# A token-major input stage, planned on five engines, in a two-layer diffusion block

## The chip, the core and the metric

The kernel runs on one core of a Trainium2 chip. Its time is the device time of one launch in microseconds (us). TensorE (PE) multiplies matrices and accumulates in PSUM; VectorE (DVE), ScalarE (ACT) and GpSimd (POOL) work on tiles in SBUF and PSUM; SyncE (SP) issues most of the loads. The profile gives, beside busy times, the clock that was granted to TensorE, as a share of full speed.

## The reference

There are 512 latent tokens `x` and 256 context tokens `ctx`, each of 1024 float32 features, and two layers. Layer 0 mixes tokens by bidirectional retention, layer 1 by HGRN2; each is followed by a convolutional GLU. What the change touches is the entry of layer 0:

```python
mod_l = silu(c) @ ada_w[0] + ada_b[0]            # shift, scale, gate, shift, scale, gate
u_l = rms_norm(x, norm_g[0, 0]) * (1 + sc1_l) + sh1_l      # and the same for ctx with c_ctx
q, k, v, g = split(u @ w_in, [1024, 2048, 4096])           # 4 heads; dk 256, dv 512
q, k = axial_rope(q), axial_rope(k)                        # latent tokens only; k scaled by 1/16
log_gamma = log_sigmoid(decay)                             # per direction and head
# chunkwise recurrence with gamma, forward and backward, context first, then
# group norm of each head, silu(g) times it, and w_out
```

Here `rms_norm` divides each token by the root of its mean square and multiplies by a gain for each feature.

## The kernel before

Activations lie feature-major: a tile has 128 features on the partitions and tokens along the free axis, in 8 feature blocks. The 768 tokens are three chunks of 256: two of latent tokens (0 and 1), then the context (2). A float32 operand is split into a high half rounded to the multiplier's format (`hi`, written by ACT) and the rest (`lo`, the operand minus `hi`, written by DVE or POOL; `split`, L93 and L94). A product is then three matmuls: hi by hi, lo by hi, hi by lo (`mm3g`, L121).

The **input stage** is what runs before the retention of head 0. SP issues its loads in program order; big ones are 1 MB each: four blocks of the scale's weights (`rada`, 1_0 to 1_3), three chunks of the transposed input `hT` (`hcin`), two blocks of the query and key weights of head 0 (`rrl`), four blocks of the shift's weights (`rada`, 0_0 to 0_3), two of the value weights of head 0 (`rv`).

- A block of the modulation vector is a PE product with silu(c) (`ada`, L216), an ACT copy to rows (L218), a PE turn to columns (`adat`, L240) and the bias (L223). From the four scale blocks DVE makes the factor `mv0A` (L341).
- A chunk is squared on ACT (L366) and summed on DVE (L368, L371); a matmul with ones sums over the features (`npshin`, L131); the reciprocal root comes from ACT (L137) and is refined on DVE (L142 to L144). DVE and POOL multiply the chunk by it (L377), ACT multiplies by `mv0A` and writes hi (L384), DVE writes lo (L385).
- The first query and key products (`ld`, L121, 288 matmuls 128x256) are made from this scaled chunk, without the shift. The shift's share of q and k is the shift times the weights (`wb`, L687, turned by `wbt`, L694), added where q and k leave PSUM: with the rotary factors for latent tokens (L780, then L781 on POOL), by ACT for the context (L792).
- Later the chunk is made again with the shift for the value product (POOL L507, then split to `ua` by L93 and L94), and the value product follows (`v`, L819, six blocks of 128 tokens with 24 matmuls each: blocks 0 and 1 read chunk 0, blocks 2 and 3 chunk 1, blocks 4 and 5 the context).

The retention then needs decay strips `T` (L742 to L754): a ramp from POOL, an exponential on ACT with the log of gamma, a mask and an addition on POOL. The log comes out of a chain of small operations on `ret_decay` (`small_params`, L174 to L207). The first consumer is `pm` on DVE (L860), scores times strip; its halves `ph` and `pl` feed the PE product `av` (L870).

In this stage ACT's order is written by hand; the orders of DVE and PE come from a scheduler that lists what the program text offers at hooks between the products, and SP is in program order. POOL's is the scheduler's too. From the retention on everything is listed by that scheduler.

A class `Plan` orders another stage already: steps with an engine, a cost, dependences and a rank go one by one to the engine that is free first on the plan's own clock, and are emitted in that order.

## Time and profile before

| | us |
|---|---|
| median of 3 runs (2180.42 to 2181.96) | 2181.53 |
| the profiled execution | 2182.16 |
| its span, first to last instruction | 2180.4 |
| PE busy | 2117.5 |
| DVE busy | 1344.1 |
| ACT busy | 832.3 |
| POOL busy | 304.3 |

The span and the profiled execution differ by 1.76 us of start and end. Mean granted clock over the span is 0.991. In the views a row of a group has its line, engine, operation, out<-in, count, busy time and mean duration in ns, and last the idle time of the engine ahead of it with what ended it; a row of a timeline has its start, its length, and the same names. Overlapping matmuls of one row are counted from the first start to the last modelled end, so a matmul's own pace is read from the distance between starts.

### The profile page before, as it was taken

What the parts mean: (1) busy time and instruction counts of PE and PEld (TensorE: products, weight loads), DVE (VectorE), ACT (ScalarE), POOL (GpSimd) and SP (SyncE); (2) the same over time, 40 slices, a digit from 0 to 9 for tenths busy, and PEclk for the clock granted to TensorE, in tenths of its full rate; (3) what the DMA queues carried; (4) which work ended last, traced back from release to release, by engine and by line L of the source; (5) the groups of instructions that cost most, each with busy time, mean ns of one, the idle gap of its engine ahead of it and who ended that gap; (6) DMA issues with size and microseconds to landing.
All of it is one profiled execution on the core that took longest, in us unless ns stands there. A gap on an engine that the chain in (4) does not pass through costs nothing. (4 is left out here: it accounts for less than half of the span.)

```text
span 2180.4 us, 30973 instructions
## 1 busy us (share of the span) xinstructions
PE 2117.5 (97%) x12416; PEld 1787.0 (82%) x12416; DVE 1344.1 (62%) x2536; ACT 832.3 (38%) x1615; POOL 304.3 (14%) x383
## 2 busy tenths in 40 slices
PE   6999999999899999999999999999999889999997
PEld 5888888888788988788888889888888668888886
DVE  6867665673523667477577576777777764334445
ACT  4543343423513633323122155434443454333323
POOL 4622040220100000000000003333333310000000
PEclk9999999999999999999999999999999999999999
DMA  9122314233133233333333532212121243232232
GB/s 296 40 77 91 113 44 141 66 119 125 40 106 116 89 116 106 111 115 118 120 113 121 188 98 86 59 40 59 40 59 40 78 167 117 94 99 97 92 112 97
DMA packets 186608, 218.25 MB, mean 100 GB/s; under 512 B 6112, under 2 KB 157664, under 8 KB 185696
## 3 DMA queue, kind: packets, MB, share of 16 engines
q1 hardware_dynamic: 179280, 196.80, 27.8%
q0 software_dynamic: 2736, 13.11, 1.6%
q10 hardware_dynamic: 4448, 6.35, 0.8%
q8 instruction: 98, 1.61, 0.3%
q14 instruction: 46, 0.38, 0.1%
HBM read 200.90 MB, written 15.34 MB: 99 GB/s over the span
## 5 line engine op out<-in xcount | busy, mean ns | idle before, releaser
L121 PE MATMUL f<-um,hua 128*128 128x512 f32 (+1 forms) x960 | 258.2, 356 | 0.0
L121 PE MATMUL f<-um,huv 128*128 128x512 f32 (+1 forms) x960 | 255.8, 354 | 0.0
L264 DVE SCALAR_TENSOR_TENSOR rows<-rada,sc,rows 128x256 f32<-128x256 f32 x504 | 231.9, 485 | 5.4
L1069 PE MATMUL f<-hd,gt 128*128 128x512 f32 x720 | 228.3, 396 | 0.0
L121 PEld LDWEIGHTS f<-um,hua 128*128 128x128 f32 x960 | 169.6, 189 | 29.4 <-issue 4.0
L121 PE MATMUL hp<-ue,hhw 128*128 128x512 f32 (+1 forms) x672 | 192.1, 373 | 0.0
L121 PEld LDWEIGHTS f<-um,huv 128*128 128x128 f32 x960 | 170.1, 189 | 25.3
L121 PE MATMUL f<-um,lua 128*128 128x512 f32 (+1 forms) x480 | 170.0, 354 | 0.0
L121 PE MATMUL f<-um,luv 128*128 128x512 f32 (+1 forms) x480 | 169.7, 354 | 0.0
L1069 PEld LDWEIGHTS f<-hd,gt 128*128 128x128 f32 x720 | 134.9, 187 | 33.6 <-issue 0.8
L1069 PE MATMUL f<-ld,gt 128*128 128x512 f32 x360 | 142.2, 395 | 0.0
L121 PEld LDWEIGHTS hp<-ue,hhw 128*128 128x128 f32 x672 | 111.9, 189 | 17.8 <-issue 1.4
L819 PE MATMUL v<-hv,ua 128*128 128x512 f32 x384 | 120.5, 390 | 0.0
L121 PE MATMUL hp<-ue,lhw 128*128 128x512 f32 (+1 forms) x336 | 120.1, 357 | 0.0
L121 PEld LDWEIGHTS f<-um,lua 128*128 128x128 f32 x480 | 90.7, 189 | 12.9
L121 PEld LDWEIGHTS f<-um,luv 128*128 128x128 f32 x480 | 90.7, 189 | 12.6
L1041 DVE TENSOR_TENSOR c<-f,c 128x512 f32<-128x512 f32 (+1 forms) x60 | 36.1, 602 | 100.9 <-PE f L121 100.8
L995 PE MATMUL wo<-hwo,ogr 128*128 128x512 f32 x288 | 89.4, 391 | 1.8 <-ACT ogr L93 1.6
L1028 ACT ACTIVATE c<-f,c_conv_b,c_conv_w 128x512 f32<-128x512 f32 (+1 forms) x60 | 42.1, 703 | 117.4 <-PE f L121 117.4
L819 PEld LDWEIGHTS v<-hv,ua 128*128 128x128 f32 x384 | 72.1, 188 | 15.4 <-issue 0.6
L94 DVE TENSOR_TENSOR lua<-rua,hua 128x512 fp32r<-128x512 f32 x80 | 50.6, 686 | 53.8 <-ACT hua L93 53.6
L451 POOL DMA_DIRECT2D h_dram<-hxe x6 | 3.2, 533 | 576.2 <-DVE yf L421 542.5
(483 smaller groups left out, 4851.9 us busy)
## 6 DMA issues: line engine op xcount, KB each, us to landing
rada<-ada_w SPq DMA_DIRECT2D x48, 1024.0 KB
rua<-ffn_w_up SPq DMA_DIRECT2D x20, 1024.0 KB
ruv<-ffn_w_up SPq DMA_DIRECT2D x20, 1024.0 KB
rd<-ffn_w_down SPq DMA_DIRECT2D x24, 768.0 KB
rhw<-hg_w_in SPq DMA_DIRECT2D x28, 512.0 KB
rv<-ret_w_in SPq DMA_DIRECT2D x8, 1024.0 KB
rg<-ret_w_in SPq DMA_DIRECT2D x8, 1024.0 KB
rqk<-ret_w_in SPq DMA_DIRECT2D x6, 1024.0 KB
```

The lines of the kernel that those rows point to most:

```text
L94: (eng or self.nc.vector).tensor_tensor(lo, raw, hi.bitcast(F32), ALU.subtract)
L121: nc.tensor.matmul(o, a, b[:, s], start=(i == 0), stop=(i == n - 1))
L264: nc.vector.scalar_tensor_tensor(rows[:, v], raw[:, k], a, rows[:, v], ALU.mult, ALU.add)
L451: nc.vector.tensor_tensor(hb(b), hb(b), yb(b), ALU.add), nc.gpsimd.dma_start(hdst[ts], hb(b))))
L819: nc.tensor.matmul(ps, a, b, start=(c == 0 and k == 0 and z == 0), stop=(c == 1 and k == 3 and z == 2))
L995: nc.tensor.matmul(ps, l, r[:, k], start=(h == 0 and k == 0 and z == 0), stop=(h == 2 and k == 3 and z == 2))
L1028: nc.scalar.activation(c[:, s], ps, AF.Identity, bias=cb[:, i, mt : mt + 1], scale=w(1))
L1041: nc.vector.tensor_tensor(c[:, s], ps, c[:, s], ALU.mult)
L1069: nc.tensor.matmul(ps, l, r[:, k], start=(k1 + k == 0 and z == 0), stop=(k1 + k == nt - 1 and z == 2))
```

## The change

The three chunks are loaded from the token-major input `h` (tokens on the partitions, rows of 4 KB); `hT` is no longer an input. The sum of squares of a token is then along the free axis: ACT squares a block of 128 tokens with an accumulated sum (L626) and takes the reciprocal root (L630), DVE refines it on one column and multiplies the identity by it (L150 to L152, L635). PE turns the chunk to feature-major by multiplying with this diagonal, which scales each token too: twelve "crosses" of four float32 matmuls 128x128 (`tri`, L653). ACT and DVE read the halves from PSUM with the factor `mv0A` (L659, L681). The matmuls with ones and the multiplications L377 go.

The context chunk gets scale and shift at once (L665, split by L671 and L675), and needs no second making. For the latent chunks the shifted version is made on DVE from the finished halves, hi + lo + shift (L778), and split again (ACT L783, DVE L784); POOL does none of it. The lo halves of the weights are all DVE's (L616, L804); POOL had taken 10 of those 16. POOL keeps the rotary additions (L871) and the strips.

All of the input stage, the rotary part and the splits of the value weights are steps of one plan over SP, PE, ACT, DVE and POOL. Steps that write one of the two small PSUM banks hold it until the step that reads it frees it. The factor `mv0A` is made in four pieces, so a chunk's first features can go ahead of the last scale block. `small_params` is called after the plan; the rotary tables are loaded through POOL's queue.

```diff
-    def run(self):
-        free = {"PE": 0.0, "ACT": 0.0, "DVE": 0.0, "SP": 0.0}
+    def run(self):
+        free = {"SP": 0.0, "PE": 0.0, "ACT": 0.0, "DVE": 0.0, "POOL": 0.0}
...
+                can = [s for s in can if not s.hold or len([t for t in back if t > now]) < self.banks]
...
-        self.fold, self.ada_b, self.norm_g, self.sel = (self.const(c) for c in ("fold", "ada_b", "norm_g", "sel"))
-        self.rsel, self.ident = self.const("rsel"), self.const("ident")
...
         nc.scalar.activation(self.sc[:, :, 0:2], cT, AF.Silu)
+        self.fold, self.ident, self.ada_b, self.norm_g, self.sel, self.rsel = (
+            self.const(c) for c in ("fold", "ident", "ada_b", "norm_g", "sel", "rsel"))
...
-    def norm_in(self, nm, chunk, hsrc, mods, u, big, tmp, late):
...
+    def first(self, u, big, tmp, rot, flat):
+        plan = Plan(2)
...
+        for n, (f, *a) in enumerate(((get_a, 1, 0), (get_x, 0), (get_w, 0), (get_a, 1, 1), (get_w, 1), (get_a, 1, 2),
+                                     (get_a, 1, 3), (get_x, 1), *((get_a, 0, c) for c in range(4)), (get_x, 2))):
+            loads[(f, *a)] = add("SP", 2.9, [], (n,), lambda f=f, a=a: f(*a))
...
+            def square():
+                ss.append(self.cp.tile([P, 1], F32, tag="iss", name=f"iss{p}{b}", bufs=6))
+                nc.scalar.activation(xs[p][:, 2], xs[p][:, b], AF.Square, accum_out=ss[0])
...
+            def diag():
+                dg.append(self.cp.tile([P, P], F32, tag="diag", name=f"idg{p}{b}", bufs=4))
+                self.newton(r[0], ss[0])
+                nc.vector.tensor_scalar(dg[0], self.ident, r[0][:, 0:1], None, ALU.mult)
...
+                def cross(j=j, ps=ps):
+                    ps.append(self.sml(f"tri{p}{j}").rearrange("p (f t) -> p f t", f=2))
+                    for f in range(2):
+                        for b, (_, dg) in enumerate(ready):
+                            k = 2 * j + f
+                            nc.tensor.matmul(ps[0][:, f, b * P : b * P + P], xs[p][:, b, k * P : k * P + P], dg[0],
+                                             start=True, stop=True)
...
+                t = add("PE", 0.45, [n for n, _ in ready] + [scale[j]] + [shift[j]] * v, (0, p, j), cross, 0.2, hold=True)
...
+                def whole(j=j, x=x):
+                    x.append(tmp(f"lt{p}{j}").rearrange("p (f t) -> p f t", f=2))
+                    for f in range(2):
+                        k = 2 * j + f
+                        h, l = self.uhl(u, k, cs)
+                        nc.vector.scalar_tensor_tensor(x[0][:, f], l.bitcast(F32), bs[:, k, v : v + 1], h.bitcast(F32),
+                                                       ALU.add, ALU.add)
...
+                n = add("DVE", 0.95, lead[p] + shift, (1, 4 + p, j), whole)
...
-            self.setup()
-            rope = []
-
-            def extra():
-                rope.extend(self.const(c, pool=rp, eng=nc.sync) for c in ("rope_row", "rope_col"))
-                self.small_params(tmp)
...
-            self.first(u, big, tmp, extra, part)
+            with tc.manual_schedule(engines={mybir.EngineType.Activation, mybir.EngineType.DVE}):
+                self.setup()
+            for n, c in ((8, "rope_row"), (64, "rope_col")):
+                rope.append(rp.tile([P, 2, 2, n], F32, name=c))
+                nc.gpsimd.dma_start(rope[-1], t[c])
+            vt = self.first(u, big, tmp, rot_steps, flat_steps)
+            self.small_params(tmp)
```

Three places show how instructions move. First SP's loads from the first to the value weights, before and then now (`x` is a chunk of `h`; `rada_125` and `rada_150` are the scale's blocks 1_0 and 1_1):

```order
L234 DMA rada_1_0_113<-ada_w 128x8x256
L234 DMA rada_1_1_114<-ada_w 128x8x256
L362 DMA hcin_117<-hT 128x8x256
...
L89 DMA c_ret_decay<-ret_decay 128x8
L89 DMA c_hg_gn<-hg_gn 128x8
L89 DMA c_ret_gn<-ret_gn 128x16
L89 DMA c_hg_lb<-hg_lb 128x16
L100 DMA rv_0_925<-ret_w_in 128x4x512
L100 DMA rv_1_937<-ret_w_in 128x4x512
```

```order
L571 DMA rada_125<-ada_w 128x8x256
L567 DMA x_127<-h 128x2x1024
L108 DMA rrl_139<-ret_w_in 128x8x256
L571 DMA rada_150<-ada_w 128x8x256
...
L567 DMA x_437<-h 128x2x1024
L108 DMA rv_0_460<-ret_w_in 128x4x512
L108 DMA rv_1_495<-ret_w_in 128x4x512
L97 DMA c_ret_decay<-ret_decay 128x8
L97 DMA c_hg_gn<-hg_gn 128x8
L97 DMA c_ret_gn<-ret_gn 128x16
L97 DMA c_hg_lb<-hg_lb 128x16
```

The first chunk is now the second big load instead of the third, and the four small tables of `small_params` stand behind both value weight loads instead of ahead of them.

Second, DVE in the changed kernel, from the last lo halves of chunk 1 to the shift (`mod`, from the turned `adat`) and the context's first features:

```order
L681 SCALAR_TENSOR_TENSOR ua_75<-tri_428,mv0A_120,ua_73 128x256 x2
L201 TENSOR_SCALAR c_hg_gn<-c_hg_gn 128x8
L202 TENSOR_SCALAR c_ret_gn<-c_ret_gn 128x16
L207 TENSOR_TENSOR lb_m<-c_hg_lb 128x8
L230 TENSOR_TENSOR mod_106<-adat_0_0_462,c_ada_b 128x4
L230 TENSOR_TENSOR mod_106<-adat_0_1_497,c_ada_b 128x4
...
L230 TENSOR_TENSOR mod_106<-adat_0_2_534,c_ada_b 128x4
L230 TENSOR_TENSOR mod_106<-adat_0_3_563,c_ada_b 128x4
L665 TENSOR_SCALAR lt_577<-tri_566,mv0A_120,mod_106 128x256 x2
```

Three operations on the small tables have moved ahead of the shift's first piece.

Third, ACT around the strips' exponentials, before and then now (`vr_4` is the eviction of the fifth value block, `T` and `tb` are the strips' parts):

```order
L743 ACT_TABLE_LOAD
L743 ACTIVATE T_0_893<-T_0_893,lg_lg 128x448 x2
...
L743 ACTIVATE tb_911<-tb_911,lg_nlg 128x320
L829 ACTIVATE vr_0_987,vs_0_988<-v_0_949 128x512
L743 ACTIVATE tb_917<-tb_917,lg_nlg 128x320
L831 ACTIVATE vh_923<-vr_0_987,vs_0_988 128x512
```

```order
L933 ACTIVATE vr_3_1129,vs_3_1130<-v_3_1104 128x512
L935 ACTIVATE vh_991<-vr_3_1129,vs_3_1130 128x512
L933 ACTIVATE vr_4_1160,vs_4_1161<-v_4_1135 128x512
L828 ACT_TABLE_LOAD
L828 ACTIVATE T_0_961<-T_0_961,lg_lg 128x448 x2
L828 ACTIVATE T_0_962<-T_0_962,lg_lg 128x320 x2
L828 ACTIVATE tb_963<-tb_963,lg_nlg 128x448
L828 ACTIVATE tb_971<-tb_971,lg_nlg 128x448
L828 ACTIVATE tb_979<-tb_979,lg_nlg 128x320
L828 ACTIVATE tb_985<-tb_985,lg_nlg 128x320
L935 ACTIVATE vh_991<-vr_4_1160,vs_4_1161 128x512
```

The exponentials of head 0's strips stood ahead of the first value block's eviction; they now stand behind the fifth's. On PE, the order from the first value matmul on is the same in both kernels.

More of the change, by code (lines that the diff above doesn't have):

```diff
@@ L61, in run @@
                     s.end = free[eng] = now + s.cost
+                    if s.hold:
+                        back.append(float("inf"))
+                    if s.frees:
+                        back.remove(float("inf"))
+                        back.append(s.end)
                     left.remove(s)
                     known.remove(s)
-            known = [s for s in left if all(d.end is not None for d in s.deps)]
-            nxt = [max(ready(s), free[s.eng]) for s in known]
-            if left:
-                now = max(now, min(nxt))
+                    moved = True
+            if left and not moved:
+                nxt = [max(ready(s), free[s.eng]) for s in left if all(d.end is not None for d in s.deps)]
+                now = min([t for t in nxt + [t for t in back if t < float("inf")] if t > now])
 class Net:
@@ L228, in ada_src @@
         return w[:, :, s * D + c * 256 : s * D + c * 256 + 256]
-    def ada_now(self, i, s, c, big):
-        nm = f"{i}_{s}_{c}"
-        raw = big([P, NF, 256], F32, "rada" + nm)
-        yield
-        self.nc.sync.dma_start(raw, self.ada_src(i, s, c))
-        yield
-        rows = self.ada_mm(nm, raw, c)
-        yield
-        pt = self.sml("adat" + nm, 4)
-        for f in range(2):
-            self.nc.tensor.matmul(pt[:, 2 * f : 2 * f + 2], rows[:, f * P : f * P + P], self.fold,
-                                  start=True, stop=True)
-        self.ada_bias(i, s, pt, slice(2 * c, 2 * c + 2))
-        yield
     def ada(self, i, s, spread=False):
@@ L768, in retention, with rot_steps, turn, flat_steps @@
         mids = deque()
-        def rot(X, h, which, j, pl, wb=None):
+        def rot_steps(j, pl, wb):
+            which, m = j // 2, j % 2
+            ab = []
+            def turn():
+                if not X0:
+                    X0.extend(big([P, 2, 2, T], F32R, f"qk{which}_0") for which in range(2))
+                p3 = pl[j].rearrange("p (r c) -> p r c", c=64)
+                tab = [(rope[0][:, which, z].unsqueeze(2) if m == 0 else rope[1][:, which, z].unsqueeze(1))
+                       .broadcast_to([P, 8, 64]) for z in range(2)]
+                ab.extend((tmp(f"ra{which}0{m}"), tmp(f"rb{which}0{m}")))
+                a3, b3 = (z.rearrange("p (r c) -> p r c", c=64) for z in ab)
+                for dst, lo, hi, z in ((a3, 0, 128, 0), (b3[0:64], 64, 128, 1), (b3[64:128], 0, 64, 1)):
+                    nc.vector.scalar_tensor_tensor(dst, p3[lo:hi], wb[lo:hi, 0:1], tab[z][lo:hi], ALU.add, ALU.mult)
+            hl = lambda z: X0[which][:, z, m, LAT]
+            return (("DVE", 2.3, turn), ("POOL", 1.5, lambda: nc.gpsimd.tensor_tensor(ab[0], ab[0], ab[1], ALU.add)),
+                    ("ACT", 0.62, lambda: nc.scalar.activation(hl(0), ab[0], AF.Copy)),
+                    ("DVE", 0.67, lambda: nc.vector.tensor_tensor(hl(1), ab[0], hl(0).bitcast(F32), ALU.subtract)))
+        def flat_steps(j, pc):
+            which, m = j // 2, j % 2
+            hl = lambda z: X0[which][:, z, m, CTX]
+            scl = (1.0, 0.0625)[which]
+            return (("ACT", 0.4, lambda: nc.scalar.activation(hl(0), pc[j], AF.Copy, scale=scl)),
+                    ("DVE", 0.45, lambda: nc.vector.scalar_tensor_tensor(hl(1), pc[j], scl, hl(0).bitcast(F32),
+                                                                         ALU.mult, ALU.subtract)))
+        def rot(X, h, which, j, pl):
             x, p3 = X[which], pl.rearrange("p (r c) -> p r c", c=64)
@@ L805, in qk, with vproj @@
             return X
[L807 removed]
+        def vproj(h, ws=None):
             vh, vl = big([P, 6, 512], F32R, f"vh{h}"), big([P, 6, 512], F32R, f"vl{h}")
             c0 = 2048 + h * 512
[L810 to L811 removed]
+            ws = ws or [self.weights(wi[:, 4 * c : 4 * c + 4, c0 : c0 + 512], 4, 512, f"v{h}_{c}") for c in range(2)]
             def mm(ps, s, c):
```

381 lines of the change are left out of this document (201 added, 180 removed).

## The prediction

> **What bounds the kernel now.** First the page's totals and slices, to see which engine sets the end and where it fails to.
>
> ```profile
> PE 2117.5 (97%) x12416; PEld 1787.0 (82%) x12416; DVE 1344.1 (62%) x2536; ACT 832.3 (38%) x1615; POOL 304.3 (14%) x383
> PE   6999999999899999999999999999999889999997
> ```
>
> TensorE is busy for 97% of the span, and its gaps lie in the first slice, in a few later ones that the change doesn't touch, and at the end. So the input stage can be worth something on its own account, and whatever reaches TensorE there goes to the end undiminished: PE's order behind it is the same in both kernels. The next view is the windows of that stage, cut at the first `ld` matmul, the first `v` matmul, the end of the third value block, the first scores and the first `av`.
>
> ```profile
> core 0: us, PE busy (x) PEld busy (x) DVE busy (x) ACT busy (x) POOL busy (x), PEclk, DMA share, GB/s
> 0.00:25.80 25.80, 11.76 (x84) 6.39 (x84) 7.80 (x17) 8.04 (x15) 5.84 (x11) 0.99 0.97 302
> 25.80:84.10 58.30, 55.37 (x448) 47.77 (x449) 51.13 (x110) 35.76 (x72) 39.13 (x42) 0.89 0.45 144
> 84.10:101.20 17.10, 16.41 (x72) 12.96 (x72) 17.05 (x24) 10.13 (x24) 12.17 (x13) 1.00 0.38 124
> 101.20:112.65 11.45, 11.45 (x52) 9.47 (x51) 8.11 (x19) 4.43 (x10) 0.45 (x1) 1.00 0.29 92
> 112.65:120.81 8.16, 8.16 (x37) 6.76 (x36) 5.35 (x10) 4.88 (x9) 0.00 (x0) 1.00 0.00 1
> ```
>
> Up to 25.8 PE is idle for 14.0 us. From there to 84.1 it lacks only 2.9, but the granted clock averages 0.89. From 84.1 DVE is full (17.05 of 17.10) and PE nearly so; from 101.2 to `av` PE has no gap. What ends PE's waits is named by the view of waits:
>
> ```profile
> PE ada L216 <- ACT sc L156: 7.5, 1, 7.5
> PE npshin L131 <- DVE hcin L371: 3.4, 2, 3.2
> PE ld L121 <- ACT ua L384: 1.9, 1, 1.9
> ```
>
> The start of the stage is a chain from loads through the norm of chunk 0 to the first product; the rest is PE's work and its clock. I therefore price three things: when `v` can start, whether DVE keeps up with it, and whether the strips are there for `av`.
>
> **When `v` starts.** The rows for the chain:
>
> ```profile
> 10.85 1.93 PE L216 MATMUL ada<-rada,sc 128*32 128x256 f32 x16 [1.43 <-DMA rada<-ada_w]
> 15.01 0.61 ACT L366 ACTIVATE hcin<-hcin 128x512 f32<-128x512 f32 x1
> 15.53 0.61 ACT L366 ACTIVATE qh3in<-hcin 128x512 f32<-128x512 f32 x1
> 16.16 1.28 ACT L137 ACT_TABLE_LOAD   x1
> 25.82 0.58 PE L121 MATMUL ld<-ua,hrl 128*128 128x256 f32 x1 [1.94 <-ACT ua L384]
> ```
>
> The second big load is usable at 10.85; now it is the first chunk. Two squares of 1024 columns at twice 0.52 (15.01 to 15.53) and a read of the accumulator each (0.19, below) make 2.5; the table load is 1.28; roots and DVE's three one-column steps with the diagonal, some 1.7; so the first cross starts near 16.3 and, on a cold PE, ends near 18. ACT has meanwhile put four weight halves of 0.52 ahead of its first read of the cross. That and DVE's lo half bring the first `ld` to about 19.5, 6.3 earlier than 25.82.
>
> PE's work changes too:
>
> ```profile
> 1804.82 1.95 PE L475 MATMUL trm<-dgm,hxm 128*128 128x128 f32 x16
> 1806.52 0.48 PE L121 MATMUL ld<-um,hfl 128*128 128x256 f32 x2
> L131 PE MATMUL npshin<-hcin,ones 128*128 128x256 f32 x12 | 4.2, 481 | 3.4 <-DVE hcin L371 3.4
> 19.72 2.98 PE L216 MATMUL ada<-rada,sc 128*32 128x256 f32 x32
> 22.63 1.25 PE L240 MATMUL adat<-c_fold,rows 128*128 128x2 f32 x8
> ```
>
> A later stage turns with the same operation: two crosses, recorded as 16 passes, take 1.70 us from start to start, so 0.85 each at full clock, where the plan's cost says 0.45. Eleven of the twelve come behind the first `ld`: +9.4. The two column sums that stood there go: about 1.0 each on a warm PE, between the 0.7 that four passes of 256 columns need and the 1.4 mean of the row: -2.0. Two of the four scale blocks with their turns, formerly done ahead of the first `ld`, now come behind it: the rows' 4.2 us for two is partly cold, half of it, 2.1, would be all warm; between them I take +3.0. Together +10.4 of work.
>
> Against it stands what PE wasted between 25.8 and 84.1: 2.9 idle, and the cold windows:
>
> ```profile
> 25.17:28.59 3.42, 2.23 (x8) 1.65 (x8) 2.83 (x5) 3.33 (x8) 2.74 (x3) 0.52 1.10 349
> 28.59:32.00 3.41, 3.41 (x15) 3.33 (x16) 3.41 (x8) 3.41 (x8) 0.00 (x0) 0.50 1.10 349
> 49.06:52.48 3.42, 1.99 (x16) 1.43 (x18) 3.42 (x11) 2.29 (x8) 0.48 (x1) 1.00 0.15 53
> 52.48:55.89 3.41, 3.41 (x25) 2.33 (x18) 3.41 (x11) 1.37 (x4) 3.04 (x4) 0.52 0.00 0
> 55.89:59.30 3.41, 3.41 (x18) 3.41 (x18) 1.42 (x7) 3.11 (x7) 3.41 (x7) 0.50 0.00 0
> ```
>
> Four windows at half clock cost four times 1.7, 6.8 with the idle time's 2.9 making 9.7. The first pair belongs to the start from idle and stays. The second pair follows a window in which PE was busy for 1.99 of 3.42; the new plan has crosses, scale blocks and `ld` to put there, and I count that pair and half of the idle as saved: -4.8. So `v` starts at 84.15 - 6.3 + 10.4 - 4.8, about 83.5. With none of the waste saved it is 88, with all of it 78.5.
>
> One new wait stands in this stretch. The four small tables are behind both value weight loads. At the 349 GB/s of the rows above a megabyte takes 3.0 us, so the fifteenth big load is there at 10.85 + 13 x 3.0, near 50, and the tables right behind it. Three DVE operations on them stand in DVE's order ahead of the shift's first piece, which frees the small PSUM bank that the third shift block on PE needs. Queued behind them are the shift, the context's crosses and all DVE work after. Chunk 2 is itself the thirteenth load, usable near 44, with 4 us of norm behind it, so the wait adds 2 to 4 us to the context's turn; PE covers it with chunk 1's products. Without that cover it would be up to 4 us more, inside the 88.
>
> **Whether DVE keeps up.** From the context's first turn (54 to 57) to the last lo half of chunk 1, DVE's order is a fixed list. Its prices are from rows that POOL didn't slow:
>
> ```profile
> 76.15 1.51 DVE L780 SCALAR_TENSOR_TENSOR rb<-ld,wb,c_rope_row 64x512 f32<-64x512 f32 x2
> 75.38 0.75 DVE L780 SCALAR_TENSOR_TENSOR ra<-ld,wb,c_rope_row 128x512 f32<-128x512 f32 x1
> 104.56 0.87 DVE L264 SCALAR_TENSOR_TENSOR rows<-rada,sc,rows 128x256 f32<-128x256 f32 x2
> 91.62 1.28 DVE L94 TENSOR_TENSOR lv<-rv,hv 128x512 fp32r<-128x512 f32 x2
> ```
>
> The context: four pairs of 256 columns at 0.87 and four lo halves at 0.64, 6.0. The shifted latent chunks: eight times (0.87 + 0.64), 12.1. Rotary: four times 2.26, 9.0. Lo halves of q and k, four, 2.6; of the value weights, eight, 5.1. Ten weighted rows of the next modulation block that are listed in between, 4.4. Small ones 2.3. Sum 41.5. Starting at 56 it ends at 97.5 if DVE never waits; each of its steps waits for PE or ACT at some point (rotary for `wb`, which is behind the context's products), and 3 to 4 us for that give 101.
>
> POOL works against this with only four additions of 1.28 us now; before, with POOL on weights and modulation, the same kind of DVE operation was stretched, as in the first row here, where 0.64 would be the unhindered price of each of three:
>
> ```profile
> 85.80 4.08 DVE L94 TENSOR_TENSOR ua<-hcin,ua 128x512 fp32r<-128x512 f32 x3
> 84.15 0.40 PE L819 MATMUL v<-hv,ua 128*128 128x512 f32 x1
> ```
>
> That is a gain of the change, and it is why the list fits at all. But chunk 1's shifted halves are last in it, and the third value block needs them. A value block is 24 matmuls in 5.45 us (17.1 - 0.7 over three), so PE asks for them 10.9 after 83.5, at 94.4, and the block would end at 99.9; with DVE's last half at 101 it ends near 102.5. Before, it ended at 101.2. So five blocks end about 1.3 to 2.5 later than at 112.65: +2, with 0 and +5 as bounds (DVE done at 97.5 or at 104).
>
> **Whether the strips are there.** Before, head 0's first strips were exponentials at 67.6, long ahead. Now ACT does them behind the eviction of the fifth value block.
>
> ```profile
> 112.85 0.60 ACT L829 ACTIVATE vr<-v 128x512 f32<-128x512 f32 x1 [2.75 <-PE v L819]
> 113.35 0.19 ACT L829 ACTIVATION_READ_ACCUMULATOR vr<-v 128x1 f32 x1
> 67.64 1.23 ACT L743 ACTIVATE T<-T,lg_lg 128x448 f32<-128x448 f32 x2
> 69.30 1.00 ACT L743 ACTIVATE T<-T,lg_lg 128x320 f32<-128x320 f32 x2
> L754 POOL TENSOR_TENSOR T<-T,tb 128x448 f32<-128x448 f32 x2 | 2.6, 1338 | 0.0
> L745 POOL TENSOR_SCALAR_AFFINE_SELECT tb<-tb 128x448 f32<-128x448 f32 x2 | 1.6, 806 | 0.0
> 114.28 0.69 DVE L860 TENSOR_TENSOR pm<-s,T 128x512 f32<-128x512 f32 x1 [0.56 <-PE s L121]
> 115.01 0.63 ACT L93 ACTIVATE ph<-pm 128x512 fp32r<-128x512 f32 x1 [0.52 <-DVE pm L860]
> ```
>
> Counted from the end of the fifth block: eviction to 0.9, table load 1.28 to 2.2, two exponentials of `T` to 4.4, two of `tb` (0.67 each) to 5.7. POOL's second mask ends near 6.6, then three additions as they are listed (1.34, 1.05, 1.34) to 10.3; `pm` and `ph` make it 11.6. PE, with the scores and the sixth value block to do, asks for `ph` 8.16 after that moment, by the last of the windows. So it stands still for 3.4. If POOL and ACT overlapped better, 2.5; if the chain of logs on DVE, which is listed between the value blocks' lo halves, is late by a microsecond, 4.5.
>
> **The sum** against the profiled execution: +2 and +3.4, and 0.6 for a window that goes cold behind one of these two stops (1.7, one time in three): +6.0, 2182.16 + 6.0 = 2188.2, or 2188. By the bounds of these terms this case runs from 2184.7 (0 + 2.5) to 2193.4 (5 + 4.5 + 1.7). The median of the runs shown lies 0.6 below the profiled execution, which I neglect.
>
> On that last term the rows and a rule differ. In the rows a window with PE busy for 1.99 of its 3.42 us, so with no window left empty, was followed by half clock. The Trainium skill, "TensorE: Matmul & The Clock Gate", Part 1: The HAM clock gate, says that the clock falls after at least one idle window of about 3.4 us; by that neither stop, of 2.5 and 3.4 us, would cool PE, and the sum would be +5.4. By the rows both can, and it would be up to +8.8. The measurement here speaks against the rule's strict reading.
>
> **Rivals.** *The early start wins (faster).* If chunk 1 never waits for the bank and nothing goes cold behind 30 us, `v` starts at 78.5. DVE must then be through with chunk 1 by 92 for the third block; its list starts when the shift is there, near 50 instead of 56 if the small tables cost nothing, and ends at 91.5 to 95. Then the fifth block ends 5.6 earlier; the strips still take 3.4: -2.2. It gets past the measurement's edge only if crosses cost the plan's 0.45 too: 12 x 0.4 = 4.8 less work, -7, near 2175. For it: POOL's pressure on DVE is gone. Against it: the cross's measured 0.85, and 41.5 us of DVE work in one line. Chance 0.13, at 2172 to 2177.
>
> *Start and stops cancel (same).* `v` at 80 to 81 instead of 83.5, DVE's list done at 96 to 97, so the fifth block ends 1 to 3 earlier than before, and the strips give it back: -1 to +3, near 2183. For it: the saved idle and cold time were counted by half. Chance 0.27.
>
> *The clock goes (much slower).* Both stops cool PE, and another wait at the bank does in chunk 1 too: 2 x 1.7 + 3.4 more, +9 to +12, near 2193. For it: the row of 1.99 of 3.42. Against it: PE is otherwise full there. Chance 0.15.
>
> *The likeliest*, +6 (2184.7 to 2191), has the rest, 0.45.
>
> A measurement of this kernel tells about 0.2%, 4.4 us, from no change. Slower by more than that are the clock's case and nearly all of the likeliest: 0.57; within it are the cancelling case and the likeliest's edge: 0.29; faster 0.14. The range that leaves out two in ten is 2179 to 2194.
>
> **What would show it.** In the profile of the changed kernel: the first cross near 16 to 17 and `ld` near 19.5; a cross at 0.85 apart from cold ones; a DVE wait for `c_hg_gn` ending near 50; the first `v` at 80 to 86; a PE stop of 2 to 4 us in the third value block ended by DVE's `ua` (L784); the fifth block's end at 113 to 117; a PE stop of about 3 us ahead of the first `av`, with ACT's table load for L828 right behind the eviction of `v_4`; and no difference behind that. The prediction is wrong if `v` starts ahead of 79, if DVE's list ends ahead of 94, or if `av` doesn't wait for the strips.

## The result and the profile after

The changed kernel takes 2193.38 us (median of 6 runs, 2191.63 to 2194.78), the kernel before beside it 2181.2 (2180.42 to 2182.0): a ratio of 1.0054, 95% interval 1.0043 to 1.0064. It is slower by 12 us. Its profiled execution took 2192.11 with a span of 2190.4, 10.0 us more span than before. Line numbers in this section are those of the changed kernel.

The totals of its page:

```profile
PE 2120.2 (97%) x12500; PEld 1791.9 (82%) x12500; DVE 1331.3 (61%) x2564; ACT 827.9 (38%) x1606; POOL 263.8 (12%) x345
```

POOL gave up 40 us and DVE 13, and PE has 2.7 more to do. None of that is 10 us. The windows of the input stage, cut as before at the first `ld` and the first `v`, then at the last of the third value block's waits, at the first scores, and around the first `av`:

```profile
core 0: us, PE busy (x) PEld busy (x) DVE busy (x) ACT busy (x) POOL busy (x), PEclk, DMA share, GB/s
0.00:21.85 21.85, 7.49 (x48) 4.53 (x49) 5.56 (x20) 9.65 (x19) 3.10 (x10) 1.00 0.95 323
21.85:81.34 59.49, 58.36 (x571) 53.06 (x570) 35.90 (x90) 24.44 (x53) 3.04 (x2) 1.00 0.46 157
81.34:98.60 17.26, 15.13 (x64) 11.14 (x62) 16.70 (x33) 6.91 (x13) 4.62 (x6) 1.00 0.32 110
98.60:112.14 13.54, 13.33 (x58) 10.92 (x59) 12.39 (x55) 7.68 (x17) 0.00 (x0) 1.00 0.25 79
122.00:130.72 8.72, 4.81 (x12) 3.52 (x13) 5.70 (x9) 2.95 (x7) 1.44 (x2) 0.61 0.36 120
```

The second row has what the change was good for: 59.49 us with 1.1 idle at a granted clock of 1.00, where in the kernel before 58.3 us had 2.9 idle at 0.89. The first `v` starts at 81.34, 2.8 earlier than at 84.15. In the third row PE is idle for 2.1 us already, and in the last one the clock is at 0.61. PE's waits up to 130 us, with the longest of each in the last column, and one of DVE's:

```profile
PE ada L224 <- DMA rada<-ada_w: 7.6, 1, 7.6
PE av L974 <- ACT ph L101: 5.4, 1, 5.4
PE tri L653 <- issue: 3.8, 1, 3.8
PE adat L592 <- ACT rows L587: 3.0, 2, 2.5
PE v L923 <- DVE ua L784: 2.1, 3, 1.0
PE v L923 <- ACT ua L783: 0.3, 1, 0.3
...
DVE c_hg_gn L201 <- DMA c_hg_gn<-hg_gn: 3.5, 1, 3.5
```

The 5.4 us is the largest wait behind the start. The timeline around it, with the first scores in its first row and those of the second score tile in its last:

```profile
112.14 2.89 PE L129 MATMUL s<-qk,qk 128*128 128x512 f32 x12
113.05 1.28 ACT L828 ACT_TABLE_LOAD   x1
114.34 2.14 ACT L828 ACTIVATE T<-T,lg_lg 128x448 f32<-128x448 f32 x4
116.39 2.12 ACT L828 ACTIVATE tb<-tb,lg_nlg 128x448 f32<-128x448 f32 x4
118.20 5.25 POOL L839 TENSOR_TENSOR T<-T,tb 128x448 f32<-128x448 f32 x4
119.83 4.76 DVE L102 TENSOR_TENSOR lqk<-rqk,hqk 128x512 fp32r<-128x512 f32 x4
124.52 0.68 DVE L964 TENSOR_TENSOR pm<-s,T 128x512 f32<-128x512 f32 x1
125.91 0.80 PE L974 MATMUL av<-ph,vh 128*128 128x512 f32 x1 [5.43 <-ACT ph L101]
130.72 0.62 PE L129 MATMUL s<-qk,qk 128*128 128x512 f32 x2
```

In the kernel before, the last of these started here:

```profile
123.53 0.39 PE L121 MATMUL s<-qk,qk 128*128 128x512 f32 x1
```

So the shift of the changed kernel against the one before is -0.5 us at the first scores (112.14 against 112.65) and +7.2 at the second (130.72 against 123.53). Of these 7.7 us, 5.4 are the stop, and most of the rest is the clock behind it: the granted clock is at half from 123.0 to 129.8, and PE works again from 125.9. Until PE stops at 120.5 the stage is level or ahead; in 18 us it loses most of what it loses at all.

Another 2.5 come in the output product of layer 0, between 589 and 713 us; from 713 us (+9.7) to the end (+9.8) nothing is added on balance. The output product begins with a wait for the gated heads (`ogr`). This is the stop ahead of it and the wait itself, before and then now:

```profile
575.66 1.22 PE L131 MATMUL rn<-sq,ones 128*128 128x256 f32 x2 [4.38 <-DVE sq L895]
589.11 0.50 PE L995 MATMUL wo<-hwo,ogr 128*128 128x512 f32 x1 [1.57 <-ACT ogr L93]
```

```profile
582.94 0.70 PE L139 MATMUL rn<-sq,ones 128*128 128x256 f32 x2 [4.44 <-DVE sq L999]
596.40 0.50 PE L1094 MATMUL wo<-hwo,ogr 128*128 128x512 f32 x1 [2.83 <-ACT ogr L101]
```

The longer wait costs nothing: it ends 13.5 us behind the stop ahead of it in both traces, and the shift is +7.3 at both places. PE only gets to it sooner, because the clock is at half for 3.4 us there (583.8 to 587.2) in place of 6.8 (574.9 to 581.7). Behind the wait the clock falls once more, from 597.4 to 600.8, which it doesn't in this trace of the kernel before, and the shift goes to +8.3. The last 1.5 come between 618 and 713 us, with no stop and at a granted clock of 1.00: PE starts fewer matmuls in the same 80 us, before and then now.

```profile
620.00:700.00 80.00, 80.00 (x355) 66.18 (x354) 16.82 (x29) 21.63 (x40) 0.00 (x0) 1.00 0.34 118
```

```profile
628.00:708.00 80.00, 80.00 (x350) 65.41 (x349) 15.61 (x28) 21.39 (x39) 0.00 (x0) 1.00 0.33 114
```

Why they are slower there is open.

### The profile page after: what moved, and what is told of

It reads as the page before. It is cut to its first block, busy times and chain, and to the rows that moved or that the text cites. A ratio compares the mean times of both kernels' runs of the same rounds, so it can differ in the third digit from the quotient of the medians.

```text
span 2190.4 us, 31127 instructions
## 1 busy us (share of the span) xinstructions
PE 2120.2 (97%) x12500; PEld 1791.9 (82%) x12500; DVE 1331.3 (61%) x2564; ACT 827.9 (38%) x1606; POOL 263.8 (12%) x345
## 5 line engine op out<-in xcount | busy, mean ns | idle before, releaser
L257 DVE SCALAR_TENSOR_TENSOR rows<-rada,sc,rows 128x256 f32<-128x256 f32 x504 | 229.2, 479 | 5.3
L129 PEld LDWEIGHTS f<-um,lua 128*128 128x128 f32 x480 | 90.7, 189 | 12.9
L923 PEld LDWEIGHTS v<-hv,ua 128*128 128x128 f32 x384 | 71.8, 188 | 19.5 <-DVE ua L784 3.6
L101 ACT ACTIVATE hua<-rua 128x512 fp32r<-128x512 f32 x80 | 44.2, 620 | 99.7 <-DMA rua<-ffn_w_up 52.3
```

What stands on the lines that cost most here:

```text
L101: self.nc.scalar.activation(hi, raw, AF.Copy)
L129: nc.tensor.matmul(o, a, b[:, s], start=(i == 0), stop=(i == n - 1))
L257: nc.vector.scalar_tensor_tensor(rows[:, v], raw[:, k], a, rows[:, v], ALU.mult, ALU.add)
L923: nc.tensor.matmul(ps, a, b, start=(c == 0 and k == 0 and z == 0), stop=(c == 1 and k == 3 and z == 2))
```

## The experiments

In the comparisons below, "the scores" are the first `s` matmul after the value product, and a shift is a start time less the same one's in the trace of the kernel before. The kernel before beside the runs had medians of 2181.2 to 2183.3.

### The small tables ahead

```diff
+            self.pre = {c: self.const(c, eng=nc.sync) for c in ("ret_decay", "hg_gn", "ret_gn", "hg_lb")}
             vt = self.first(u, big, tmp, rot_steps, flat_steps)
...
-        dec = self.const("ret_decay", eng=nc.sync)
+        dec = self.pre["ret_decay"]
```

> The changed kernel with the four small table loads issued ahead of the input stage's loads; nothing else moves by hand. In the changed kernel DVE waits 3.5 us for them (until 48.37) and PE stops 0.99 us at 44.07. Theory (PE's own work sets the start of v, the wait was covered): the first v matmul comes 1 us earlier than 81.34, the third value block's stop and the 5.4 us stop ahead of av stay, the time falls by 0 to 1.5 us. Rival (the wait sets when DVE's list begins): the list begins 3 us earlier than 56.65, the stops of 2.4 us in the third value block go, the time falls by 3 to 4 us.

2193.33 us (2191.83 to 2195.4), ratio 1.0057 (1.0042 to 1.0072): no gain. DVE's wait for the table near 48 us is gone, the stops of 2.4 and 5.4 stand unchanged, and the four loads ahead make the first big load later:

```profile
PE ada L224 <- DMA rada<-ada_w: 9.2, 1, 9.2
```

7.6 became 9.2, but the first cross came only 0.1 later (16.90 against 16.80). The first `v`, forecast 1 us earlier, came 2.0 later, and so did the scores (114.15). Of these 2 us the span, 2191.9, shows 1.5 and the median none; as much differs between two executions of one program (below), so they can't be laid to the loads. The wait was covered by PE's other work, as the prediction said. The rival, by which the wait costs its time, falls.

### The lo halves of the next weights on POOL

`lqk`, the lo halves of the second head's query weights, stands on DVE ahead of `pm`. Here POOL makes them, behind the strips.

```diff
-                wh, wl = self.weights(wi[:, :, col0 + c : col0 + c + 256], NF, 256, f"{name}{c}")
+                wh, wl = self.weights(wi[:, :, col0 + c : col0 + c + 256], NF, 256, f"{name}{c}", eng)
...
-                     lambda j, pl, pc, which=which: epi(which, j, pl, pc))
+                     lambda j, pl, pc, which=which: epi(which, j, pl, pc), nc.gpsimd if h == 1 and which == 0 else None)
```

> The changed kernel with the lo halves of head 1's first query weights (lqk, four of 128x512) made by POOL instead of DVE. Theory (two causes at av: the strips come late, and DVE has lqk ahead of pm, stretched to 4.76 us beside POOL's additions): pm starts right after the strips' third addition, near 121.5 to 122.3 instead of 124.52, the stop ahead of av falls from 5.4 to about 3, the time by 2 to 3 us, more if no window goes cold. Rival (the strips alone set it): the stop stays within 0.5 us of 5.4 and the time within 1 us.

2192.85 us (2191.77 to 2193.81), ratio 1.0054 (1.0039 to 1.0069). The first `pm`, the waits and the window behind them:

```profile
122.10 0.69 DVE L964 TENSOR_TENSOR pm<-s,T 128x512 f32<-128x512 f32 x1 [1.85 <-POOL T L839]
...
PE av L974 <- ACT ph L101: 2.7, 1, 2.7
PE av L974 <- DVE pl L102: 0.4, 1, 0.4
...
123.00:131.00 8.00, 7.08 (x18) 5.24 (x19) 4.24 (x5) 2.39 (x5) 5.73 (x4) 0.57 0.13 33
```

The stop is 3.1 in place of 5.4, and DVE now waits for the strips ahead of `pm`. That settles the stop's parts: some 3 us are the strips, as predicted, and the rest is `lqk` on DVE ahead of `pm`. But the shorter stop cooled PE as well, at 0.57 over these 8 us. The second score tile started at 129.58, 1.1 earlier, and the median moved by 0.5, less than the 2 to 3 us that the theory had put on it.

### The logs of gamma ahead of the plan

`small_params` is called ahead of the plan; only its last two operations, which write the logs, stay behind chunk 1's halves, so that the strips can't start too early.

```diff
+            self.small_params(tmp)
             vt = self.first(u, big, tmp, rot_steps, flat_steps)
-            self.small_params(tmp)
...
+        add("DVE", 0.5, [us[1][3]], (0, 1, 9), lambda: self.lg_fin())
```

> The changed kernel with the chain of logs run at the start, in DVE's idle time, and its last two operations behind chunk 1's turn, so that ACT's first exponentials of the strips come near 45 and the rest ahead of the first value evictions. Theory (the strips' place behind the fifth value block costs the 5.4 us stop and the 2.1 us of cold clock behind it): no stop ahead of av, no cold window there, the first av near 120 instead of 125.9, the time 7 to 8 us below the changed kernel's, about 2185 to 2186, with 1 us either way from the tables. Rival (DVE is simply overloaded there and the stop moves elsewhere): the logs' 40 small operations and three more ACT table loads delay the first ld or the third value block by 3 us or more, and the time falls by less than 4.

2195.96 us (2193.58 to 2197.94), ratio 1.0068 (1.0053 to 1.0083). The stop ahead of `av` is gone; the stop at the third value block grew instead, and PE cooled twice:

```profile
PE v L931 <- DVE ua L792: 5.2, 3, 4.1
...
49.00:56.00 7.00, 6.36 (x31) 6.36 (x31) 0.16 (x1) 4.81 (x10) 0.05 (x1) 0.51 0.04 15
107.00:114.00 7.00, 4.89 (x12) 3.85 (x13) 6.69 (x16) 1.51 (x4) 0.72 (x1) 0.51 0.00 0
```

ACT now made the strips' exponentials, with their table load, from 45.9 to 49.3, ahead of the copies for the shift. PE stopped for 2.7 us at 46.9, the clock fell, and the first `v` came at 87.76, 6.4 later than in the changed kernel. The strips' additions on POOL ran between 103 and 108, beside DVE's list, and there the second stop arose. The scores came at 124.63. The rival held: the loss moved to other places, half of it ahead of `v` and half to the block where DVE is the bound.

### Each cross twice

Every cross is computed two times into the same place, which leaves the result as it is.

```diff
+                            for _ in range(2):
+                                nc.tensor.matmul(ps[0][:, f, b * P : b * P + P], xs[p][:, b, k * P : k * P + P], dg[0],
+                                                 start=True, stop=True)
```

> The changed kernel with every matmul of the twelve crosses issued twice (the second overwrites the first). Theory (PE is the bound from the first cross to the first v, a cross is 0.85 us of it): the first v matmul comes 12 x 0.85 = 10.2 us later than 81.34, near 91; DVE's list begins later by some 8, so the stops in the third value block stay; the end moves by 8 to 10 us, to 2201 to 2204. Rival (the crosses lie beside waits for data or DVE, so their number is nearly free): v moves by less than 5 us and the time by less than 4.

2204.5 us (2203.7 to 2205.07), ratio 1.0106 (1.0089 to 1.0123). The crosses between 20 and 80 us, here and then in the changed kernel:

```profile
L654 PE MATMUL tri<-idg,x 128*128 128x128 f32 x180 | 22.0, 277 | 1.3 <-DVE ua L682 1.3
```

```profile
L653 PE MATMUL tri<-idg,x 128*128 128x128 f32 x88 | 11.1, 277 | 0.0
```

The added crosses are 10.9 us of PE in this stretch; the scores came 12.9 later than in the changed kernel's first trace, and the median is 11.1 higher, half a microsecond above the theory's range. The stops of 2.4 and 5.4 stayed. So up to the value product PE is the bound, and a microsecond put on it there comes out at the end almost whole.

### The logs through POOL's queue, then rotary later too

As the third experiment, but with the four tables loaded through POOL's queue and the last two operations behind all of chunk 1's halves, so that no strip runs beside DVE's list. The second of the two kernels also ranks the last rotary piece behind the shifted halves.

```diff
-        dec = self.const("ret_decay", eng=nc.sync)
+        dec = self.const("ret_decay", eng=nc.gpsimd)
...
-        add("DVE", 0.5, [us[1][3]], (0, 1, 9), lambda: self.lg_fin())
+        add("DVE", 0.5, ends, (9, 9), lambda: self.lg_fin())
...
-                n = [add(eng, cost, n, (1, j), f)]
+                n = [add(eng, cost, n, (1, j if j < 3 else 9), f)]
```

> The changed kernel with the small tables loaded by POOL's queue at the start, the chain of logs run in DVE's idle time there, and its last two operations listed behind chunk 1's last lo half, so that ACT makes head 0's strips between the evictions of the second and third value blocks and POOL adds them near 105 to 111. Theory (the strips' place costs the 5.4 us stop and the cold window behind it, and the run with the logs early failed because ACT's exponentials stood ahead of the shift's copies near 47 and POOL's additions beside DVE's list near 100): first v within 1 us of 81.3, stops in the third block of 2 to 3 us as in the changed kernel, none ahead of av, first av near 120.5, the time 7 to 8 us below the changed kernel's, 2185 to 2187. Rival (ACT is too full there: three table loads and the exponentials hold back the evictions, so that PE waits for PSUM in blocks four to six): stops of 2 to 4 us move there, the time falls by less than 4.

> The run before this one in the list, with the fourth rotary step ranked behind chunk 1's shifted halves, so that these come 2 to 3 us earlier in DVE's list. Theory (the third block's stops come from these halves being last in DVE's list): the stops of 2.4 us go, the fifth block ends 2 to 2.5 us earlier than in the run before, the time falls by as much, to 2183 to 2184.5. Rival (a later value block needs the PSUM bank that the fourth rotary step frees): the stop moves to the fourth block, the time within 1 us of the run before.

2192.21 us (2191.96 to 2192.45), ratio 1.0049 (1.0034 to 1.0064), and 2192.57 (2191.24 to 2192.87), ratio 1.0049 (1.0033 to 1.0066). In the first of them there is no stop ahead of `av` and no cold window, and its scores and second scores stand at

```profile
118.70 2.89 PE L129 MATMUL s<-qk,qk 128*128 128x512 f32 x12
129.67 1.56 PE L129 MATMUL s<-qk,qk 128*128 128x512 f32 x6
```

with shifts of +6.05 and +6.14 (against 112.65 and 123.53): the 7.7 us between those places are gone, as the theory had it. They were spent at the start instead:

```profile
PE tri L660 <- issue: 8.6, 1, 8.6
PE adat L599 <- ACT rows L594: 5.2, 2, 4.7
```

The first cross waited 8.6 in place of 3.8, since ACT did the exponential and the logarithm of the chain, with their table loads, ahead of the squares of chunk 0, and one more exponential with a table load between these and the roots. In the second kernel one stop of 1.84 us in the third value block took the place of the several short ones, the clock went cold behind it (105.8 to 109.2), and the scores came at 118.76: nothing won, where the theory had the stops gone and 2 us or more.

### The same kernels again

> The kernel before, profiled once more. In its first trace PE's clock is halved from 574.5 to 581.5, ahead of the output product of layer 0, and full in that product's first stretch (589 to 600); in all five traces of changed kernels it is also halved for 3.4 us there, and 2.4 to 2.9 us are lost between 124 and 713. Theory (where the free-running windows fall decides it): this trace may show either, and its place of loss is the clock alone. Rival (the change makes it, by another order or load there): full clock there again, and no loss against the first trace.

> The changed kernel, profiled once more. Theory (clock windows): the stops of 2.4 and 5.4 us are the same to 0.2 us, the cold window behind av and the one near 597 to 601 may lie otherwise, and the distance to the kernel before differs by 1 to 3 us from the first trace's accordingly. Rival (fixed by the change): both windows as in the first trace to a window's width.

The kernel before gave 2183.52, 1.4 us more span than its first trace; the changed one 2194.8, 2.7 more span than its first. In the kernel before, the output product went cold this time behind a wait of 2.2 us for the gated heads:

```profile
589.00:594.00 5.00, 4.90 (x14) 3.72 (x15) 5.00 (x8) 5.00 (x10) 0.00 (x0) 0.66 0.02 3
```

That cost 1.0 us; it had been 1.0 ahead of its first trace up to there, and its 1.4 us more of span come from clock windows behind 1700 us. Of the traces shown here only its first one has no cold window at this place, so that loss isn't the change's. The 1.5 us between 618 and 713 are another matter: here they are 0.0. From 640 to 713 us all eleven traces with the new input stage lose 1.0 to 1.1, and the other two with the old one nothing.

In the changed kernel the waits were the same to 0.1 us from the third value block on, and the cold windows lay behind the same stops as in its first trace, which is what the rival said. But the scores came at 114.67, 2.5 later. The difference arose at the start. The stretch from 20 to 30 us, in the first trace and then in the second:

```profile
20.00:30.00 10.00, 9.48 (x97) 7.35 (x90) 4.81 (x12) 3.74 (x9) 0.00 (x0) 1.00 1.08 366
```

```profile
20.00:30.00 10.00, 9.50 (x74) 7.67 (x63) 4.64 (x11) 4.00 (x9) 0.00 (x0) 1.00 1.08 364
```

PE was busy for the same 9.5 us and did 97 matmuls in one and 74 in the other: it ran at full pace from about 21 us in the one and from 26.3 in the other. The clock column says 1.00 in both. So up to 2.5 us here and 1.0 at the output product differ from execution to execution of one program; no argument on the change may rest on them. The medians are over several executions and average this.

### The chain of logs in the gaps

The tables come through POOL's queue again. Now the chain is cut into steps of the plan: DVE's first part where it waits anyway, ACT's functions behind the last copy of the shift's rows, DVE's long part behind chunk 1's last halves.

```diff
+        n = add("DVE", 1.4, [loads[get_a, 0, 1]], (0, 5), lambda: self.lgp[0](), lag)
+        n = add("ACT", 3.3, [n, rcopy[0, 3]], (-2,), lambda: self.lgp[1]())
+        add("DVE", 6.0, ends + [n], (0, 0, -9), lambda: self.lgp[2]())
...
-            self.small_params(tmp)
+            self.lgp[3]()
```

> The changed kernel with the small tables loaded by POOL's queue, the chain of logs in three pieces: its first DVE operations near 37 to 45, ACT's exponentials and logarithm between the last shift copy and the context's halves (52 to 56, where ACT is idle), the rest of the chain behind chunk 1's last lo half. Theory (what cost 6.5 us in the two runs with the logs at the start was ACT's table loads ahead of chunk 0's squares, and what the strips cost is 7.7): first v within 1 us of 81.3, third block's stops 2.4 as in the changed kernel, the exponentials 3 us earlier than 114.34, the stop ahead of av 0 to 2.5 instead of 5.4, the time 4 to 7.5 us below the changed kernel's 2193.4. Rival (table loads cost there too, and the stop moves to the context's halves): first v 3 us later or more, no gain.

2188.11 us (2186.01 to 2189.65, 11 runs), ratio 1.0028 (1.0019 to 1.0037): 5.3 less than the changed kernel. PE's waits between the first value block and the second scores, and these scores (this kernel's line numbers):

```profile
PE v L941 <- DVE ua L798: 2.0, 3, 0.8
PE av L992 <- DVE pl L102: 1.0, 1, 1.0
...
125.26 0.39 PE L129 MATMUL s<-qk,qk 128*128 128x512 f32 x1
```

The stop at `av` is 1.0, no cold window follows, the scores stand at 112.71 (+0.1) and the second scores at 125.26 (+1.7, where the changed kernel has +7.2). The end is at +4.1, for the output product cost 2.4 again. So where the strips' logs are made explains about half of the loss (5.3 of 12.2 in the medians), with the clock that fell behind it.

### The weighing later

Between the shifted halves DVE has weighted rows of the next modulation block (L257). In this kernel that block is queued behind the second head's query product. The same was done to the kernel before.

```diff
-        for s in (2, 4, 3):
-            self.ada(0, s, True)
...
                 q, k = qk(h + 1)
+                if h == 0:
+                    for s in (2, 4, 3):
+                        self.ada(0, s, True)
```

> The run before this one in the list, with the next modulation block's loads and weighted rows listed behind head 1's query and key projection, which takes 10 DVE operations (4.3 us) out of DVE's list between 84 and 99 and lets the chain of logs end earlier. Theory (DVE's list sets the third value block): its stops of 2.4 us go, no stop ahead of av, the scores 2.5 us earlier than 112.1, and the time 2 to 3 us below the run before, at 2179 to 2183, level with the kernel before or a little below it. Rival (POOL's rotary additions or ACT set the third block): stops of 1.5 us or more stay, the time within 1 us of the run before.

> The kernel before with the same move of the next modulation block alone. Theory (there DVE is full from 84 to 101 but PE waits only 0.7 us for it, so taking work from DVE is worth nothing on PE): within 1 us of the kernel before. Rival (the move is worth 2 us by itself, whatever the input stage): 2 us or more below it.

2189.9 us (2189.57 to 2194.85, 5 runs), ratio 1.0042 (1.0029 to 1.0055), and 2191.48 (2191.08 to 2194.02, 5 runs), ratio 1.0046 (1.0033 to 1.0059). In the first, with the new input stage and the logs in the gaps:

```profile
50.00:100.00 50.00, 49.87 (x398) 43.85 (x397) 42.69 (x96) 22.82 (x45) 7.56 (x8) 1.00 0.13 43
100.00:150.00 50.00, 50.00 (x242) 42.18 (x241) 30.91 (x74) 27.08 (x51) 16.34 (x24) 1.00 0.20 64
622.00:632.00 10.00, 3.65 (x9) 2.98 (x10) 0.42 (x2) 0.00 (x0) 0.00 (x0) 0.50 0.71 263
...
PE adat L288 <- DMA arow<-ascr: 8.9, 1, 8.9
```

From 50 to 150 us PE has no stop left, and the same `av` matmul that starts at 526.95 in the kernel before starts at 521.19, a shift of -5.8. In the kernel before the same edit moves that matmul to 525.90, -1.05. With this edit in both, the new input stage is thus 4.7 us ahead of the old one, in one trace each. Then both lose 13 to 15 us by 713, some 12 of it in one place: the modulation's last block is now so late that its rows aren't back from memory when PE asks. That stop is 8.9 us (9.0 in the old stage), and the clock, at half for 10.2 us, stays there for some 4 us behind it. Neither time was foreseen: the theory had 2179 to 2183 for the first, and both it and its rival had the second level with the kernel before or below it.

### The weighing later by one place less

The block is queued ahead of the second head's query product, one filler slot earlier.

```diff
+                if h == 0:
+                    for s in (2, 4, 3):
+                        self.ada(0, s, True)
                 st = strips(h + 1)
                 q, k = qk(h + 1)
-                if h == 0:
-                    for s in (2, 4, 3):
-                        self.ada(0, s, True)
```

> As e10_weighing_later, but the twelve fillers of the modulation sums are queued before the second head's queries and keys, not behind them, so that each is one slot earlier and the last product stands 72 matmuls of the output product ahead of the one that reads its rows back from memory. Theory (e10 lost what it had won only to that read: the 8.9-us stop and the cold clock of 622 to 632 behind it, together 13 us between its shift of -5.8 at 527 us and +7.4 at the end): the stop goes, the shift at 527 us stays at -5 to -6, the span comes to 2174 to 2178 us, the time to 2175 to 2180, under the kernel before. Rival (the output product's start is where every gain goes: a stop of 2 to 3 us on the gated heads and cold windows of 2 to 5 us follow whatever comes ahead): no 8.9-us stop, but the shift is -2 to +3 at the end and the time 2181 to 2186. A third way: the first weighings now stand beside the second head's query product or the strips, and a stop of 2 us or more shows between 130 and 200 us, with the shift at 527 us above -4.

2179.86 us (2178.2 to 2184.49, 11 runs), the kernel before beside it 2183.32 (2179.16 to 2184.51, 15 runs): ratio 0.9994, 0.9985 to 1.0003.

```profile
580.00:600.00 20.00, 17.13 (x76) 13.69 (x75) 15.87 (x20) 12.75 (x19) 0.00 (x0) 0.91 0.16 54
600.00:640.00 40.00, 40.00 (x182) 32.22 (x180) 6.77 (x12) 10.22 (x19) 0.00 (x0) 1.00 0.27 93
```

The late read is gone (no stop from 600 to 640), and with it 10 us against the previous experiment's 2189.9. The shift is -4.6 at 527 and -1.3 at 713, behind the output product's start. The median is within the theory's 2175 to 2180; the profiled execution (2182.66, span 2180.9) lies in the rival's range and its end is level with the first trace of the kernel before, +0.1. So the late read cost about what the theory said, and the output product still ate 3 us of the gain, of the size that the rival said: the cold window behind the wait for the gated heads is in it, and the slower matmuls behind 618 us. No difference from the kernel before is shown: the interval holds 1. Three places had to be put right to come level again. The kernel before with the modulation block queued here too was not run, so what this place is worth to the old stage isn't known.

## Why the prediction was right in its direction and too small

The forecast was 2188, the time 2193.4, inside the range and outside the likeliest case's own 2184.7 to 2191. Against the three terms of the sum:

- **The fifth value block, +2 predicted: -0.5 measured, +2.0 in the second trace.** `ld` started at 21.85 instead of 19.5, because a scale block's product (1.76 us) stands on PE between the first crosses and it. Against that, `v` started at 81.34 instead of 83.5. The step "I count that pair and half of the idle as saved: -4.8" was too careful for this trace: there is no cold window between 21.85 and 81.34 and only 1.1 us of idle time. Taking all of the waste as saved gives 58.3 + 10.4 - 9.7 = 59.0, and the row has 59.49. The cross at 0.85 is confirmed by the experiment with each twice. But some 2.5 us of this term hang on how soon PE gets warm at the start: in the second trace `v` started at 83.86 and the scores at 114.67, so that the +2 came true there. The term was right to within what differs between executions.
- **DVE's list**, 56 to 101, ran from 56.65 to 100.2, and the stops it makes in the third value block are 2.4 us; with `v` 2.2 earlier, its end and not the start of `v` set that block's end, as the step said. The wait for `c_hg_gn` ended at 48.37, predicted near 50, and covered, predicted so.
- **The strips, +3.4 predicted: 5.4 measured.** The chain was worked out rightly: table load, exponentials and additions, the third addition done near 122.2, which alone would be a stop of about 3, as the experiment with `lqk` on POOL shows. Left out was DVE: `pm` is queued behind four `lqk` operations that were 2.5 us before and 4.76 here. The sum followed the producer of the operand and not the queue of the engine that reads it. `lqk` is long here because it runs beside POOL's additions, the very stretching that the prediction quoted as a thing of the kernel before and counted as gone.
- **The clock, +0.6 predicted: about 2 measured behind the stop.** "One time in three" was wrong for a stop of that length: the clock fell in all four traces with a stop of 5.4 us (both traces of the changed one, the tables ahead, each cross twice), and also with 3.1 us.
- **Behind that, nothing predicted: 2.5 measured.** "No difference behind that" had no step at all and failed. 1.0 of it is the cold window at the output product, which the kernel before has in its second trace too. 1.5 are the slower matmuls between 618 and 713 us, which only the new input stage has. Why it has them, and why the medians differ by 2 us more than the first profiles, stays open.

The case with the clock, at 2193, had the right time, but in part by luck: of its mechanism, the cold behind the strips' stop is shown; the one behind the stops in the third value block and the one at the bank did not occur.

The clock can be held against more rows now. Its changes lie on a grid of 3.41 us in every trace. Behind 5.4 us of standing still, longer than such a window, PE is cold; but 1.84 us did it too, in the experiment with rotary later, and the 3.1 of the one with `lqk` on POOL. The Trainium skill, "TensorE: Matmul & The Clock Gate", Part 1: The HAM clock gate, has the clock fall after at least one idle window of about 3.4 us. The stop of 1.84 us speaks against that as a condition. Laid on the grid, the window ahead of its cold one still has 1.6 us of busy PE; the stops of 2.4 us in the changed kernel are spread over two windows that have 2.3 and 2.2, and nothing fell there. In the fourteen traces every fall of the clock follows a window with PE busy for at most 2.0 of its 3.41 us. That is no threshold: with the tables ahead, a window with 1.5 us busy was followed by full clock. The same section says that the window runs freely and isn't reset by the kernel's start, so that the point of warming varies between runs, by 500 ns either way. The 97 and 74 matmuls in the same ten microseconds agree with that in kind; but the two traces got warm about 5 us apart.

Why `lqk` was long can be read from two groups: the additions with `lqk` on POOL, behind them, and `lqk` with the logs through POOL's queue, where the additions were over:

```profile
L839 POOL TENSOR_TENSOR T<-T,tb 128x448 f32<-128x448 f32 (+1 forms) x4 | 4.3, 1113 | 0.0
```

```profile
L102 DVE TENSOR_TENSOR lqk<-rqk,hqk 128x512 fp32r<-128x512 f32 x4 | 2.5, 687 | 0.5 <-ACT hqk L101 0.5
```

Apart, the additions take 4.3 us and the four `lqk` 2.5; together they took 5.25 and 4.76. From the first addition to the last `lqk` pass 6.4 us, close to the 6.8 that both need one behind the other. The Trainium skill, "SBUF — State Buffer", Who interferes with whom, says that a DVE operation with two SBUF inputs contends with a POOL operation that reads SBUF, and that the ports they share are held by one at a time. The 6.4 us against 6.8 nearly agree with that.

## What to carry to other kernels

A chain's end is not when its operand is ready but when the engine that reads it gets there: price what stands in that engine's queue, at the price it has beside what else runs then. When work leaves an engine ahead of a stage and lands behind it, look for the next consumer that has no slack (here the strips, then DVE's list, then a modulation block), since undoing one stop moved it to the next three times. Changes of a few microseconds at the entry of a long TensorE-bound program meet clock windows that differ by as much from execution to execution; judge them by the shift at places in between, over two traces, and only then by the end.

## What was not expected

- A stop of 1.84 us on PE was followed by 3.4 us at half clock (105.8 to 109.2), while four stops of at most 1.0 each, 2.4 in all, in the same block were not.
- The clock column shows 1.00 at the start of a trace while matmuls still run at half pace: 74 of them in 9.50 busy us in one execution, 97 in 9.48 in another.
- The kernel before, in the runs beside the last experiment, fell into two groups, 2179.2 to 2181.4 and 2183.3 to 2184.5. What makes the groups was not found; its two traces differ by 1.0 to 1.4 us at each of three places, the start, the output product and behind 1700 us.
